# Low parts of weights by accumulating DMAs onto negated high parts

## The chip, the core and the metric

The kernel runs on one core of a Trainium2 chip. TensorE (PE), VectorE (DVE), ScalarE (ACT), GpSimd (POOL) and SyncE (SP) each run their own queue of instructions in order and wait for each other by semaphores; DMA queues move data between the device memory and the core. The metric is the time of one execution on the device in microseconds (us), as the median of several runs.

## What is computed

Two layers of an encoder over 768 tokens (512 of one request, 256 of another; the weights are shared) with 1024 channels. Each layer normalises its input, runs three token mixers on it, gates, projects and merges them, and adds the result:

```
h = rmsnorm(x, g_pre) * (1 + scale) + shift
cq, ckv, kr, gate_a, qkv_b, gate_b, qkv_c, gate_c, merge = split(h @ w_in)
p_a = (mla_attention(cq, ckv, kr, ...) * silu(gate_a)) @ w_pa        # branch A
p_b = (dilated_attention(rope(q_b), rope(k_b), v_b) * silu(gate_b)) @ w_pb   # branch B
p_c = (neighbourhood_attention(q_c, k_c, v_c, rpb) * silu(gate_c)) @ w_pc    # branch C
mg = sigmoid(merge)
mixed = mg[0] * p_a + mg[1] * p_b + mg[2] * p_c
x = x + gate * rmsnorm(mixed @ w_out, g_post)
```

All arrays are float32.

## The kernel before

Every product of two float32 matrices is made of three passes of PE on numbers rounded to float32r: high part times high part, weight's high part times activation's low part, weight's low part times activation's high part. The high part is the value rounded, the low part is what the rounding left off. So each weight tile needs a high and a low copy in SBUF before PE can use it.

`load_split` makes them. SP loads a raw tile of up to 1024 columns into one of three buffers (`WR`). Then, in pieces of 512 columns, ACT casts the piece into a slot `hi` of the ring `WH` (line 175), and `sub_lo` subtracts: `lo = raw - hi`, into a slot of the ring `WL` (line 158, the helper's line). Each ring has four slots of 512 columns, that is two full tiles. `sub_lo` goes to DVE, except that in some phases every n-th call goes to POOL: `LO_POOL = dict(l=2, m=3, p=1)` says every second call of phase "l" (latents of branch A), every third of "m" (branches B and C of the merge) and all of "p" (output projection). `sub_lo` also makes low parts of activations, so line 158 stands for more than weights: `lo<-ox` is the split of a branch's output in the merge.

A tile of a feature (`feat_mm`, line 199) is 48 matmuls: eight pieces of the contraction, three passes, two groups of tokens. Its products are named after the user: `qkb` (branch B), `qc` and `kc` (branch C), `gate`, `mg` (merge gates). `value_group` and `value_pair` (lines 722 and 741) make the values `vp`. In the merge each of 24 steps runs a merge gate `mg`, unless it was made ahead during the branches (`early`, then it is loaded back from `th_scr`), and 24 matmuls `pp` of the projection (line 1051), whose weights are one piece of 512 or 256 columns (`w_pj`). DVE multiplies the two (line 1060), POOL adds into `mixed` (line 1062). The merge of layer 0 also computes the conditioning vectors on DVE (`ada_tile`, line 309, on tiles `tm`).

The softmax of branches A and C (`soft_keys`) goes round the engines: DVE takes the maximum over the tiles (lines 650 and 652), POOL reduces it over the partitions (line 653), DVE subtracts (658), ACT takes the exponential (659), and the same for the sum. `pv` then splits the weights: ACT casts (667), DVE subtracts (668), PE multiplies with the values (671). Branch B does the same at lines 841 to 890.

The order on each engine is fixed when the kernel is built: a scheduler places the instructions of the program on the engines' queues, so that tiles of the next products are loaded and split under the current ones.

Of the kernel before, what the change touches and what calls it, by code (L numbers as in the profile page):

```python
# [15 lines left out]
AF = mybir.ActivationFunctionType  # L16
ALU = mybir.AluOpType
# [29 lines left out]
NW = (0, 64, 192, 256)  # L47


LO_POOL = dict(l=2, m=3, p=1)  # L50

FILL = ((2, 0, 1, 0, 2, 3, 1, 0, 1, 1, 1, 1, 0, 0, 0, 0, 0, 0, 0, 0, 0), (5, 0, 2, 3, 0, 4, 0, 1, 1, 1, 1, 2, 1, 0, 0, 0, 0, 0, 1, 0, 0))

# [10 lines left out]
def trunk_kernel(ctx, tc, x_t, c_row, c_col, w_ada0, w_ada, cols, w_a, w_feat, w_val, w_val2, w_uqk, w_qr, w_uv, w_pj, w_o,  # L64
                 bias_s, bias_p, rope_t, rope_k, mask_b, mask_c, y_t):
    nc = tc.nc
# [18 lines left out]
    def U(tag, dt=F32, name=None):  # L85
        return pool.tile([P, T], dt, tag=tag, name=name or tag, bufs=BUFS[tag])
# [11 lines left out]
    def ring(name):  # L98

        n, width = RINGS[name]  # L100
        t = part[name]
        state = dict(i=0)

        def take():
            i = state["i"]
            state["i"] = (i + 1) % n
            return t[:, i * width:(i + 1) * width]
        return take
# [8 lines left out]
    def Z4(name):  # L117
        return Z4_().rearrange("p (k g) -> p k g", g=2)

    def f(ap):  # L120
        return ap.bitcast(F32)
# [24 lines left out]
    state = dict(lo=0, pz=0, phase="l")  # L146
# [5 lines left out]
    def sub_lo(out, a, b, eng=None):  # L152

        if eng is None:
            state["lo"] += 1
            every = LO_POOL.get(state["phase"])
            eng = nc.gpsimd if every and state["lo"] % every == 0 else nc.vector
        eng.tensor_sub(out, a, b)  # L158

    def load_split(src, n, keep=None, ring=None):  # L160

        raw = WR()
        state["dma"] = nc.sync.dma_start(out=raw[:, :n], in_=src)
        parts = []
        w = 384 if keep else 1024 if ring else 512
        for o in range(0, n, w):
            m = min(w, n - o)
            if keep:
                t = U(keep, F32R)
                hi, lo = t[:, :w], t[:, w:]  # L170
            elif ring:
                hi, lo = ring(), ring()
            else:
                hi, lo = WH(), WL()
            nc.scalar.copy(hi[:, :m], raw[:, o:o + m])  # L175
            sub_lo(lo[:, :m], raw[:, o:o + m], f(hi[:, :m]))
            parts.append((hi, lo))
        return w // P, parts

# [386 lines left out]
    def branch_a(l, h_, h):  # L566
# [14 lines left out]
        for pr in range(4):  # L581
            early(l, h, FILL[l][1 + 2 * pr])
            if pr % 2 == 0:
# [17 lines left out]
                nc.scalar.activation(qr_hl[0], qr, AF.Copy, scale=scale)  # L601
                nc.vector.scalar_tensor_tensor(qr_hl[1], qr, scale, f(qr_hl[0]), ALU.mult, ALU.subtract)
            parts = load_split(w_uqk[l, pr], 640)
            qo = feat_mm(None, 3, cqn, name="qn", parts=parts)
            qn = []
# [575 lines left out]
    c = Z4("c")  # L1181
# [8 lines left out]
    for t_ in range(T // P):  # L1190
        x, x2 = U("cv", name="x"), x2s[t_ // 3][:, t_ % 3 * 256:t_ % 3 * 256 + 256]
        nc.sync.dma_start(out=x, in_=x_t[t_, :, :T])
        if t_ % 3 == 0:
            nc.sync.dma_start(out=x2s[t_ // 3].rearrange("p (t c) -> p t c", c=256),
                              in_=x_t[t_:t_ + 3, :, T:].rearrange("t p c -> p t c"))
# [208 lines left out]
```

## Time and profile before

| | |
|---|---|
| median of 3 runs | 1976.61 us (1974.0 to 1978.97) |
| profiled execution, its own time | 1972.72 us |
| span of the profile, first to last instruction | 1970.9 us |
| PE busy | 1848.2 us, 94% of the span |
| DVE busy | 1555.8 us, 79% |
| ACT busy | 1016.3 us, 52% |
| POOL busy | 645.1 us, 33% |

The profile gives, for one execution, when each instruction ran and what released it. Busy is the time in which an engine executed; what is left of the span is idle. The clock that TensorE was granted is 0.977 of its full speed as a mean. The stages below are cut at the places where the first matmuls of a branch begin; neighbouring branches overlap a little at the cuts.

### The profile page before, as it was taken

Reading aid. Unit: us, or ns where it says so; the run is one execution under the profiler, and the core shown is the slowest. Engines: PE = TensorE matmul, PEld = TensorE weight load, DVE = VectorE, ACT = ScalarE, POOL = GpSimd, SP = SyncE. Lnnn points to the kernel's source line nnn. Section 1 sums busy time; section 2 is a strip of 40 time slices with the busy share of each in tenths; the row PEclk is TensorE's granted clock in tenths of the full one; section 3 lists DMA queues with packets and bytes.
Section 4 is the critical chain, followed back from the end, with each engine's and each line's share of the span. In section 5 each row is a group of like instructions: output and inputs, shape, how many; then the busy total and the mean of one; then the engine's idle time right before and its main releaser. Section 6 shows DMA issues by size and latency. Waiting matters only on the chain.

```text
span 1970.9 us, 30150 instructions
## 1 busy us (share of the span) xinstructions
PE 1848.2 (94%) x10674; PEld 1641.7 (83%) x10674; DVE 1555.8 (79%) x3016; ACT 1016.3 (52%) x2121; POOL 645.1 (33%) x428
## 2 busy tenths in 40 slices
PE   7999899999989989998799999999999999988998
PEld 7987789988868878887699888889888878876898
DVE  8557779599978998999985258787699868997763
ACT  5456466456684555222364356574566674553241
POOL 6404334012121555026532014343022211454570
PEclk9999999999999989999899999999999999998999
DMA  8142231232212243557431332422323222233652
GB/s 294 65 125 73 81 118 62 92 101 79 92 46 97 79 145 118 192 171 241 143 132 52 103 118 87 136 82 68 105 76 94 84 70 97 87 105 100 210 180 70
DMA packets 94536, 220.20 MB, mean 112 GB/s; under 512 B 17984, under 2 KB 32392, under 8 KB 94384
## 3 DMA queue, kind: packets, MB, share of 16 engines
q1 hardware_dynamic: 89776, 211.97, 33.0%
q10 hardware_dynamic: 4608, 6.29, 1.1%
q8 instruction: 84, 1.38, 0.3%
q14 instruction: 68, 0.56, 0.1%
HBM read 172.73 MB, written 28.18 MB: 102 GB/s over the span
## 4 chain that ended last, share of the span: by engine, by line
PE 58%; DVE 24%; issue 6%; ACT 5%; DMA 4%; POOL 2%; SPq 0%; DVEq 0%; ACTq 0%; POOLq 0%
PE mg L199 15%; PE qkb L199 6%; PE op L1152 6%; PE vp L741 4%; PE pp L1051 4%; PE gate L199 4%; DVE fixed L668 3%; DVE fixed L158 3%; PE cq L547 3%; DVE fixed L309 2%; PE sp L632 2%; PE ck L547 2%; DVE tq L658 2%; PE vp L722 2%; PE qc L199 2%
## 5 line engine op out<-in xcount | busy, mean ns | idle before, releaser
L653 POOL PARTITION_ALL_REDUCE fixed<-fixed x128 | 305.5, 2413 | 516.0 <-DVE fixed L650 317.4
L199 PE MATMUL mg<-fixed 128*128 128x512 f32 (+1 forms) x2304 | 439.2, 343 | 0.7 <-DVE u L435 0.5
L199 PEld LDWEIGHTS mg<-fixed 128*128 128x128 f32 x2304 | 363.0, 192 | 52.0 <-DVE u L435 0.9
L175 ACT CAST fixed<-fixed 128x512 fp32r<-128x512 f32 (+1 forms) x332 | 199.3, 606 | 314.7 <-PE mg L199 103.8
L158 DVE TENSOR_TENSOR fixed<-fixed,fixed 128x512 fp32r<-128x512 f32 (+3 forms) x309 | 234.7, 764 | 96.5 <-ACT fixed L175 93.4
L199 PE MATMUL qkb<-fixed 128*128 128x512 f32 (+1 forms) x1152 | 211.5, 338 | 0.0
L199 PEld LDWEIGHTS qkb<-fixed 128*128 128x128 f32 x1152 | 176.9, 189 | 23.9
L199 PE MATMUL gate<-fixed 128*128 128x512 f32 (+1 forms) x960 | 185.5, 343 | 6.5 <-DVE fixed L158 4.4
L1051 PE MATMUL pp<-hi,fixed 128*128 128x512 f32 (+1 forms) x640 | 165.4, 347 | 8.9 <-DVE fixed L158 5.6
L199 PEld LDWEIGHTS gate<-fixed 128*128 128x128 f32 x960 | 150.5, 192 | 27.3 <-DVE fixed L158 4.9
L1051 PEld LDWEIGHTS pp<-hi,fixed 128*128 128x128 f32 x640 | 114.0, 195 | 26.4 <-DVE fixed L158 7.1
L668 DVE TENSOR_TENSOR fixed<-tq,fixed 128x512 fp32r<-128x512 f32 (+1 forms) x160 | 133.3, 855 | 1.5 <-ACT fixed L667 1.3
L659 ACT ACTIVATE tq<-tq 128x512 f32<-128x512 f32 (+1 forms) x160 | 83.4, 546 | 79.9 <-DVE tq L658 79.4
L1051 PE MATMUL pp<-lo,fixed 128*128 128x512 f32 (+1 forms) x320 | 110.8, 347 | 2.3 <-DVE lo L158 1.8
L658 DVE TENSOR_TENSOR tq<-tq,fixed 128x512 f32<-128x512 f32 (+1 forms) x160 | 100.3, 675 | 14.6 <-POOL fixed L653 14.2
L1152 PE MATMUL op<-wo,fixed 128*128 128x384 f32 (+1 forms) x648 | 108.6, 322 | 2.0 <-DVE fixed L1125 2.0
L309 DVE SCALAR_TENSOR_TENSOR fixed<-tm,fixed 128x768 f32<-128x768 f32 (+1 forms) x128 | 106.8, 834 | 2.0
L1152 PEld LDWEIGHTS op<-wo,fixed 128*128 128x128 f32 x648 | 103.0, 191 | 2.4 <-DVE fixed L1125 2.4
L424 POOL MEMSET kb<- 64x768 f32 x56 | 41.1, 735 | 166.5 <-PE sp L808 60.9
L856 POOL PARTITION_ALL_REDUCE fixed<-fixed x16 | 46.1, 2899 | 142.6 <-DVE fixed L833 75.2
L650 DVE TENSOR_TENSOR fixed<-tq 128x256 f32<-128x256 f32 (+1 forms) x128 | 78.2, 614 | 10.9 <-ACT tq L635 5.7
L667 ACT CAST fixed<-tq 128x512 fp32r<-128x512 f32 (+1 forms) x160 | 81.2, 531 | 8.8 <-PE o_ps L671 6.0
(244 smaller groups left out, 3884.9 us busy)
## 6 DMA issues: line engine op xcount, KB each, us to landing
fixed<-in_w_feat_dram SPq DMA_DIRECT2D x108, 512.0 KB
tm<-in_w_ada_dram SPq DMA_DIRECT2D x42, 384.0 KB
th_scr<-the SPq DMA_DIRECT2D x35, 384.0 KB
th<-th_scr SPq DMA_DIRECT2D x35, 384.0 KB
fixed<-in_w_val_dram SPq DMA_DIRECT2D x20, 512.0 KB
xs<-xb SPq DMA_DIRECT2D x96, 96.0 KB
fixed<-in_w_pj_dram SPq DMA_DIRECT2D x32, 256.0 KB
fixed<-in_w_o_dram SPq DMA_DIRECT2D x16, 512.0 KB
```

The costliest lines, as they stand in the source:

```text
L158: eng.tensor_sub(out, a, b)
L175: nc.scalar.copy(hi[:, :m], raw[:, o:o + m])
L199: state["mm"] = nc.tensor.matmul(outs[g], w[:, wsl], a[g], start=(i == 0 and wi == 0), stop=(i == nk - 1 and wi == 2))
L309: nc.vector.scalar_tensor_tensor(junk, x, 1.0, c, ALU.mult, ALU.mult, accum_out=ada2[:, l, i, g, j:j + 1])
L547: mm = nc.tensor.matmul(ps[t][c], hl[a][g][:, k, c0:c0 + P], w[k][c][b], start=(i == 0 and j == 0), stop=(i == KT - 1 and j == 2))
L653: nc.gpsimd.partition_all_reduce(red, out, P, RED.max if op == ALU.max else RED.add)
L658: nc.vector.tensor_sub(x, x, m)
L659: nc.scalar.activation(x, x, AF.Exp)
L667: nc.scalar.copy(hi, x)
L668: nc.vector.tensor_sub(lo, x, f(hi))
L1051: nc.tensor.matmul(pp, w[:, ws], o[k][a][:, o_:o_ + n], start=(i == 0), stop=(i == 3 * nk - 1))
L1152: mm = nc.tensor.matmul(op[cc], m[a][g][:, k, c0:c0 + P], parts[k][cc][b], start=(k == 0 and i == 0), stop=(k == KT - 1 and i == 2))
```

## The change

In the phases "b", "c", "m0" and "m" (branch B, branch C, first and later branches of the merge) a weight's low part is no longer made by `sub_lo`. ACT writes the negated rounded value, `lo = -raw`, rounded to float32r by the write, which is the negated high part. Then a DMA issued from POOL reads the same weights from the device memory a second time and adds them to `lo` in place, so that `lo = raw - hi`. ACT writes `hi` as before. The tiles with `keep` (output projection) and the other phases stay as they were. "m" leaves `LO_POOL`, so all `lo<-ox` are on DVE. The new names are line 178 (negation), 179 (the DMA) and 180 (cast); later lines are 7 higher than before.

```diff
--- before.py
+++ after.py
@@ -47,7 +47,9 @@
 NW = (0, 64, 192, 256)
 
 
-LO_POOL = dict(l=2, m=3, p=1)
+LO_POOL = dict(l=2, p=1)
+
+LO_DMA = ("b", "c", "m0", "m")
 
 FILL = ((2, 0, 1, 0, 2, 3, 1, 0, 1, 1, 1, 1, 0, 0, 0, 0, 0, 0, 0, 0, 0), (5, 0, 2, 3, 0, 4, 0, 1, 1, 1, 1, 2, 1, 0, 0, 0, 0, 0, 1, 0, 0))
 
@@ -172,8 +174,13 @@
                 hi, lo = ring(), ring()
             else:
                 hi, lo = WH(), WL()
-            nc.scalar.copy(hi[:, :m], raw[:, o:o + m])
-            sub_lo(lo[:, :m], raw[:, o:o + m], f(hi[:, :m]))
+            if not keep and state["phase"] in LO_DMA:
+                nc.scalar.activation(lo[:, :m], raw[:, o:o + m], AF.Copy, scale=-1.0)
+                nc.gpsimd.dma_start(out=lo[:, :m], in_=src[:, o:o + m], accum_op=ALU.add)
+                nc.scalar.copy(hi[:, :m], raw[:, o:o + m])
+            else:
+                nc.scalar.copy(hi[:, :m], raw[:, o:o + m])
+                sub_lo(lo[:, :m], raw[:, o:o + m], f(hi[:, :m]))
             parts.append((hi, lo))
         return w // P, parts
```

The lists of the built programs say what stands where. The old one has 309 weight subtractions of rings `WH` and `WL` on DVE: 288 of 128x512, 9 of 128x256, 4 of 128x384 and 8 of 128x128. In the new one 73 of 128x512 are left and none of 128x256, and POOL has 236 DMAs: 148 of `w_feat`, 40 of `w_val` (all 128x512) and 48 of `w_pj` (32 of 128x512, 16 of 128x256).

DVE in the merge of layer 0, between two steps (`fixed_72` holds the rounded tiles, `fixed_73` the plain ones; `tm` is the conditioning work). Before:

```order
L1060 SCALAR_TENSOR_TENSOR mixed<-th,pp 128x256
L309 SCALAR_TENSOR_TENSOR fixed_73<-tm,fixed_73 128x256
L158 TENSOR_TENSOR fixed_72<-fixed_73,fixed_72 128x512
L311 TENSOR_TENSOR fixed_73<-fixed_73 128x2
L309 SCALAR_TENSOR_TENSOR fixed_73<-tm,fixed_73 128x768
L309 SCALAR_TENSOR_TENSOR fixed_73<-tm,fixed_73 128x256
L309 SCALAR_TENSOR_TENSOR fixed_73<-tm,fixed_73 128x768
L309 SCALAR_TENSOR_TENSOR fixed_73<-tm,fixed_73 128x256
L158 TENSOR_TENSOR fixed_72<-fixed_73,fixed_72 128x512
L311 TENSOR_TENSOR fixed_73<-fixed_73 128x2
L309 SCALAR_TENSOR_TENSOR fixed_73<-tm,fixed_73 128x768
```
The same place in the changed kernel:

```order
L1067 SCALAR_TENSOR_TENSOR mixed<-th,pp 128x512
L316 SCALAR_TENSOR_TENSOR fixed_73<-tm,fixed_73 128x256
L316 SCALAR_TENSOR_TENSOR fixed_73<-tm,fixed_73 128x768
L1067 SCALAR_TENSOR_TENSOR mixed<-th,pp 128x256
L316 SCALAR_TENSOR_TENSOR fixed_73<-tm,fixed_73 128x256
L318 TENSOR_TENSOR fixed_73<-fixed_73 128x2
L316 SCALAR_TENSOR_TENSOR fixed_73<-tm,fixed_73 128x768
L316 SCALAR_TENSOR_TENSOR fixed_73<-tm,fixed_73 128x256
L316 SCALAR_TENSOR_TENSOR fixed_73<-tm,fixed_73 128x768
L316 SCALAR_TENSOR_TENSOR fixed_73<-tm,fixed_73 128x256
L318 TENSOR_TENSOR fixed_73<-fixed_73 128x2
```
The subtraction that stood between the conditioning rows (`L158`) is gone, and nothing stands in its place.

ACT in branch C of layer 0, in a stretch with the exponentials (line 659, later 666) and casts (667, later 674) of the softmax. Before:

```order
L175 CAST fixed_72<-fixed_73 128x512
L404 ACTIVATE qs<-qc_6817 64x64
L961 DMA fixed_73<-in_bias_p_dram 128x512
L659 ACTIVATE tq<-tq 128x512 x2
L667 CAST fixed_72<-tq 128x512 x2
L175 CAST fixed_72<-fixed_73 128x512
L416 CAST ka<-kc_6886 64x512
L417 CAST ka<-kc_6886 64x512
L416 CAST ka<-kc_6887 64x256
L417 CAST ka<-kc_6887 64x256
L659 ACTIVATE tq<-tq 128x256 x2
L667 CAST fixed_72<-tq 128x256 x2
L175 CAST fixed_72<-fixed_73 128x512
```
And a stretch of the same branch in the changed kernel:

```order
L666 ACTIVATE tq<-tq 128x512
L180 CAST fixed_72<-fixed_73 128x512
L178 ACTIVATE fixed_72<-fixed_73 128x512
L666 ACTIVATE tq<-tq 128x512
L674 CAST fixed_72<-tq 128x512 x2
L180 CAST fixed_72<-fixed_73 128x512
L178 ACTIVATE fixed_72<-fixed_73 128x512
L666 ACTIVATE tq<-tq 128x256 x2
L674 CAST fixed_72<-tq 128x256 x2
L180 CAST fixed_72<-fixed_73 128x512
L178 ACTIVATE fixed_72<-fixed_73 128x512
```
Each cast of a weight piece is followed, at once or some instructions later, by the negation `L178`; the scheduler has put the cast first.

POOL from the end of branch C to the merge of layer 1 (`L653`, later `L660`, are the softmax's all-reduces; a bare `ISA` row is a change of POOL's program). Before:

```order
L653 ISA fixed_73<-fixed_73 128x512
L653 ISA fixed_73<-fixed_73 128x256
L158 ISA
L158 TENSOR_TENSOR lo<-ox,hi 128x768
L653 ISA
L653 ISA fixed_73<-fixed_73 128x512
L653 ISA fixed_73<-fixed_73 128x256
L653 ISA fixed_73<-fixed_73 128x512 x2
L653 ISA fixed_73<-fixed_73 128x256 x2
L653 ISA fixed_73<-fixed_73 128x512
L653 ISA fixed_73<-fixed_73 128x256
L158 ISA
```
The changed kernel:

```order
L179 DMA fixed_72<-in_w_pj_dram 128x512
L660 ISA fixed_73<-fixed_73 128x512
L179 DMA fixed_72<-in_w_pj_dram 128x512
L660 ISA fixed_73<-fixed_73 128x256
L179 DMA fixed_72<-in_w_pj_dram 128x512
L660 ISA fixed_73<-fixed_73 128x512
L179 DMA fixed_72<-in_w_pj_dram 128x512
L660 ISA fixed_73<-fixed_73 128x256
L179 DMA fixed_72<-in_w_pj_dram 128x512 x2
L179 DMA fixed_72<-in_w_pj_dram 128x256 x5
L1069 ISA
L1069 TENSOR_TENSOR mixed<-mixed,th 128x768
```
The two changes of program around the single `lo<-ox` are gone, and a DMA stands between most of the all-reduces.

## Rows read from the trace of the kernel before

**Rows 1.** The page: span, busy time of the engines, the chain by engine.

```profile
span 1970.9 us, 30150 instructions
...
PE 1848.2 (94%) x10674; PEld 1641.7 (83%) x10674; DVE 1555.8 (79%) x3016; ACT 1016.3 (52%) x2121; POOL 645.1 (33%) x428
...
PE 58%; DVE 24%; issue 6%; ACT 5%; DMA 4%; POOL 2%; SPq 0%; DVEq 0%; ACTq 0%; POOLq 0%
```

**Rows 2.** B0, C0, M0, B1, C1, M1: length; busy PE, PEld, DVE, ACT, POOL; clock; DMA.

```profile
300.00:545.00 245.00, 238.58 (x1384) 213.63 (x1382) 209.23 (x365) 141.60 (x272) 53.31 (x32) 0.99 0.27 85
545.00:760.00 215.00, 193.15 (x1077) 165.34 (x1076) 191.17 (x349) 128.62 (x255) 81.10 (x42) 0.96 0.29 93
760.00:955.00 195.00, 172.85 (x941) 148.85 (x940) 184.32 (x388) 55.78 (x110) 76.92 (x43) 0.94 0.55 184
1320.00:1567.00 247.00, 240.19 (x1415) 215.19 (x1414) 211.79 (x368) 139.27 (x272) 58.73 (x32) 1.00 0.27 85
1567.00:1806.00 239.00, 216.80 (x1200) 185.16 (x1198) 193.32 (x353) 138.99 (x273) 78.69 (x42) 0.96 0.28 89
1806.00:1896.00 90.00, 85.48 (x475) 73.83 (x476) 73.84 (x104) 31.88 (x62) 54.86 (x34) 0.96 0.60 193
```

**Rows 3.** PE's waits in C0, C1 and M0: us, times, longest.

```profile
PE o_ps L671 <- DVE fixed L668: 4.9, 3, 1.9
...
PE o_ps L877 <- DVE fixed L158: 1.1, 3, 0.6
...
PE o_ps L671 <- DVE fixed L668: 8.9, 7, 2.1
PE o_ps L671 <- ACT fixed L667: 5.2, 1, 5.2
...
PE o_ps L671 <- DVE o_t L392: 0.6, 1, 0.6
...
PE op L1152 <- DVE th L1060: 12.1, 2, 11.4
PE pp L1051 <- DVE fixed L158: 5.6, 3, 2.0
```

**Rows 4.** Groups by line and shape, whole span: weight subtractions and casts.

```profile
L158 DVE TENSOR_TENSOR fixed<-fixed,fixed 128x512 fp32r<-128x512 f32 x288 | 223.8, 780 | 91.1 <-ACT fixed L175 88.1
L175 ACT CAST fixed<-fixed 128x512 fp32r<-128x512 f32 x300 | 184.7, 620 | 280.0 <-PE mg L199 89.5 <-PE qkb L199 45.5 <-DMA fixed<-in_w_pj_dram 27.4
...
L158 DVE TENSOR_TENSOR lo<-ox,hi 128x768 fp32r<-128x768 f32 x15 | 16.0, 1080 | 0.1
```

**Rows 5.** DVE's timeline in M0: start, us, then what.

```profile
885.58 0.41 DVE L158 TENSOR_TENSOR fixed<-fixed,fixed 128x256 fp32r<-128x256 f32 x1
...
889.79 2.02 DVE L158 TENSOR_TENSOR fixed<-fixed,fixed 128x256 fp32r<-128x256 f32 x1
```

**Rows 6.** POOL's timeline in M0 and at the end of C1.

```profile
889.00 2.53 POOL L1062 TENSOR_TENSOR mixed<-mixed,th 128x768 f32<-128x768 f32 x1 [1.30 <-DVE fixed L311]
...
1786.18 1.84 POOL L158 TENSOR_TENSOR lo<-ox,hi 128x768 fp32r<-128x768 f32 x1 [6.98 <-DVE fixed L678]
1794.50 2.87 POOL L653 PARTITION_ALL_REDUCE fixed<-fixed  x2 [6.48 <-issue]
```

**Rows 7.** The chain in order of time, in M0 and M1: start, us, what.

```profile
785.01 8.48 PE mg L199 x48
793.49 4.18 PE pp L1051 x24
...
1858.63 2.82 DMA fixed<-in_w_pj_dram
```

**Rows 8.** Groups of POOL in C0.

```profile
L653 POOL PARTITION_ALL_REDUCE fixed<-fixed x28 | 64.3, 2313 | 95.3 <-DVE fixed L650 89.8 <-DMA den_scr<-fixed 3.2 <-issue 1.6
```

**Rows 9.** The page's DMA queues: packets, MB, share of 16 engines.

```profile
q1 hardware_dynamic: 89776, 211.97, 33.0%
```

**Rows 10.** Groups of DVE in M0.

```profile
L158 DVE TENSOR_TENSOR fixed<-fixed,fixed 128x512 fp32r<-128x512 f32 x28 | 29.0, 1036 | 0.4 <-ACT fixed L175 0.4
```

## Prediction

> **What bounds the kernel now.** I read the page first: TensorE (PE) is busy 1848.2 us of a span of 1970.9 us, VectorE (DVE) 1555.8, ScalarE (ACT) 1016.3, GpSimd (POOL) 645.1 [rows 1]. The chain that ended last runs 58% through PE and 24% through DVE [rows 1]: PE is the bound, and where it stands still DVE mostly ends the wait. So at most PE's idle time can be won, and only in the stages that the change touches. I cut the span into stages (B is branch B, C branch C, M the merge, 0 and 1 the layers) and took length less PE busy [rows 2]: B0 6.4 us, C0 21.9, M0 22.2, B1 6.8, C1 22.2, M1 4.5, together 84 us. In the same rows DVE is busy 85% of B0, 89% of C0, 95% of M0, 86% of B1, 81% of C1 and 82% of M1, ACT never more than 60%. The reader is to see two kinds of stage: in B PE hardly waits although DVE is full; in C and at the end of M0 it waits for a full DVE. The waits say so [rows 3]: in C0 PE waits longest for the low part of the softmax weights (DVE L668, 4.9 us), in C1 too (8.9), and in M0 for the th product (DVE L1060) 12.1 and the weights' subtraction (DVE L158) 5.6. These low parts of weights (L158) rarely hold PE themselves; they take DVE's time ahead of work that does.
>
> **What goes.** DVE does 288 subtractions of 128x512 at 780 ns [rows 4]; by the order lists 73 are left, so 215 go: 167.7 us. Nine of 128x256 go too, some 0.41 us each [rows 5]: 4 us. The counter for POOL no longer exists in the merge, so 5 subtractions of lo<-ox come to DVE at 1.08 us [rows 4]: back 5 us. DVE loses 166 us, 11% of its work, all in the six stages. It also loses waits: L158 stood 91 us behind ACT's cast [rows 4], and everything on DVE behind it stood too (not all of it in these stages). POOL loses 17 subtractions (5 of 128x512, 7 of 128x256, 5 of lo<-ox), none longer than the 1.84 us of a lo<-ox [rows 6]: at most 31 us. And it loses two changes of program, the bare ISA rows in the order lists. One of them shows: at 1786.18 POOL does one lo<-ox of 1.84 us, and then stands 6.48 us, waiting for nothing that the profile names, before the two all-reduces that follow [rows 6]. PE waits 5.2 us for ACT in C1, once [rows 3], at 1799, behind those all-reduces.
>
> **What is added.** ACT negates 220 pieces of 128x512 and 16 of 128x256. The nearest row is its own cast, 620 ns [rows 4]; 236 of these are at most 146 us, and ACT goes from 52% to 59%. POOL issues 236 accumulating DMAs (B0 46, C0 32, M0 46, B1 50, C1 34, M1 28, counted from the tiles that each stage loads and summing to the list's 236). The trace has no DMA from POOL. What an issue holds POOL for lies between nothing (issues of SP and ACT are not counted as busy at all) and an all-reduce, 2.3 us [rows 8]; I take 1.2, the middle, since neither is nearer. The transfer is 256 KB. A plain one of that size stands for 2.82 us on the chain [rows 7]; this one also has to read the old content, so twice that, 5.6, is the upper end; I take 5, near the upper end. No DMA is added to SP's queue, which keeps its loads in a slightly altered order.
>
> **Is the low part in time?** A ring has four half tiles. PE takes 8.48 us for a tile of two halves and 4.18 for the merge's projection half [rows 7], so a slot that PE has freed is needed again after three others, 3 x 4.2 = 12.7 us. In that time now go the cast 0.62, the negation 0.62, the issue 1.2 and the landing 5: 7.4 us; with both upper ends 0.62 + 0.62 + 2.3 + 5.6 = 9.1. Both fit, with 3.6 to 5.3 us left for a queue on ACT or POOL. So where tile follows tile (all of B, most of M0) the transfers cost nothing: they lie under PE's own matmuls. That cover is gone where the raw load comes late: ACT waited 27.4 us for loads of w_pj [rows 4], in the merges. There a half is cast and used at once, and cast + subtraction = 1.4 us turns into 7.4. PE waited 5.6 us, 3 times, for L158 in M0 [rows 3]; each gets up to 6 us worse, 18 in all, of which I charge half, as the DVE that also held these products is freer.
>
> **The merge's DVE.** At 885.58 a subtraction of 128x256 takes 0.41 us, and the same at 889.79 takes 2.02 us [rows 5], while POOL adds two SBUF tiles into mixed from 889.00 for 2.53 us [rows 6]. So POOL's own subtractions cost DVE time as well, and they go; its adds stay. The open question is whether POOL's DMA issues slow DVE as its adds do. I count them as not, but if all 46 of M0 did, by the 1.61 us between those two rows, DVE would get back 74 us where it loses some 29 (28 subtractions of 128x512 at 1036 ns [rows 10]). The Trainium skill (SBUF — State Buffer, Who interferes with whom) has a rule for this: a DVE instruction with two SBUF inputs contends with a GpSimd instruction that reads SBUF, not with one that only writes. By that rule adds would slow DVE, as these rows agree, and issues, which write descriptors, would not; the term stays as counted.
>
> **Sum**, against the profiled execution's own 1972.7 us: C0 and C1, 44 us idle, of which 28 end on DVE (six kinds of wait in C0 from 4.9 us down to 1.1, four in C1 from 8.9 down to 0.6 [rows 3]). DVE loses 32 + 34 subtractions there, one for each DMA, at 0.78 us: 51 of 384 us busy, 13%, and the waits on the cast; I let half of the 28 go: -14. The program change at the end of C1: -6. M0: of 22 us, 15 go with the freer DVE and 9 come back by late loads: -6. B0 and B1, 13 us idle, a third: -4. M1: 0. ACT's 146 us lie mostly under idle time; a twentieth of them on the path of the softmax: +7, less 3 for DVE's freed waits: +4. Sum -26, so 1946.7. The median of the runs shown is 3.9 us above the profiled run: **1950 us**.
>
> **Rivals.** *More is won.* If DVE's queue was behind almost all of PE's waits, C gives 28 and M0 20: with the 6 and 4 it is -58, 1918. For it: DVE at 89 to 95%. Against: a softmax chain goes through DVE, POOL, DVE, ACT, DVE and PE in turn, and a wait in it does not vanish when DVE is free.
> *POOL becomes the queue* (slower). The order lists put a DMA straight before an all-reduce some 17 times in each C. Such a DMA waits for ACT's negation, which waits for PE to free the slot, and the all-reduce waits behind it, then DVE's tq, ACT's exp and PE's o_ps. At 2.3 us for 34 of them, 78 us; PE has gates and merge tiles to fill in with, so half is seen: +39. With -26 it is +13, 1990. It decides from 26 / 17 = 1.5 us of delay for each. For it: POOL's issues stand in line with the one engine that all heads pass. Against: POOL waits for DVE's partial results in C0 more than it works (64.3 us busy and 95.3 idle before these 28 all-reduces [rows 8]).
> *Landing is far longer than 5.6 us.* Above 12.7 - 2.4 = 10.3 us every half is late; at 11.5 us, 1.2 us for some 200 halves: +240, less the gain, 2190. Against: nothing in the trace takes so long.
> *It is hidden, or DMA eats it* (no change). The added 58.4 MB at the rate of the page (212 MB for 33.0% of the engines [rows 9]) are 9% of the span's DMA; M0 and M1 stand at 55% and 60% [rows 2], and 46 pieces in M0 add 10.7 MB to some 36, so it goes to 71%, and to 88% if each byte counts twice. If the loads of w_pj come so much later that ACT's 27.4 us double, that cancels the gain. The Trainium skill (Collectives: The Full Stack, The bandwidth ceiling) says that a DMA that adds needs two source reads and runs at about half the rate of a copy; by it the 88% holds. No row here has such a DMA.
>
> **How the numbers follow.** A difference of 0.3%, 6 us, is about what a measurement of this kernel can tell. Chances: the forecast (10 to 45 us won) 0.48; more won 0.13; no change 0.14; POOL's queue 0.18; late landing 0.07. Faster 0.61, same 0.14, slower 0.25. The range reaches up to the POOL rival and down to the larger gain, and leaves out the late landing and the tails: 1918 to 1992.
>
> **What would show it.** Right: 73 subtractions of 128x512 on DVE in place of 288, PE's idle in C0 and C1 each under 17 us, no 6.48 us gap on POOL at the end of C1, PE's waits for a DMA into fixed under 15 us in all. Wrong: PE waiting for lo from POOL's queue in B (then landing is long), POOL all-reduces that start late with DVE's partial result long done (POOL's queue), ACT's waits for w_pj far above 27 us (DMA), or DVE subtractions and adds of 2 us outside the merge's adds (the issues slow DVE).

## The result: slower by 1.2%

The changed kernel takes 2000.37 us (median of 4 runs, 1997.14 to 2004.62), the kernel before 1977.79 (4 runs beside them, 1974.0 to 1980.24). The ratio is 1.0119, 95% interval 1.0101 to 1.0136. That is outside the range, on its slow side. The profiled execution took 2001.39 us.

The page of the changed kernel: busy time, DMA queues, chain, groups of instructions, DMA issues (KB each, median us to landing).

```profile
span 1999.6 us, 30560 instructions
...
PE 1860.8 (93%) x10674; PEld 1641.9 (82%) x10674; DVE 1417.6 (71%) x2797; ACT 1135.7 (57%) x2357; POOL 809.9 (41%) x647
...
q1 hardware_dynamic: 89776, 211.97, 32.8%
q0 software_dynamic: 33984, 59.78, 18.2%
...
PE 32%; DVE 12%; DMA 6%; ACT 5%; issue 4%; POOL 2%; SPq 1%; ACTq 0%; DVEq 0%; POOLq 0%
...
L179 POOL DMA_DIRECT2D fixed<-in_w_feat_dram x148 | 131.0, 899 | 373.6 <-ACT fixed L178 247.2
...
L178 ACT ACTIVATE fixed<-fixed 128x512 fp32r<-128x512 f32 (+1 forms) x236 | 145.3, 616 | 26.9 <-PE vp L748 23.8
...
fixed<-in_w_feat_dram POOLq DMA_DIRECT2D x148, 256.0 KB, 4.7
...
fixed<-in_w_val_dram POOLq DMA_DIRECT2D x40, 256.0 KB, 5.0
```

Against [rows 1] VectorE gave back 138 us (166 were predicted; without the DMAs, in e4_no_dma below, it is 152), ScalarE took 119 more, and PE is busy 12.6 us *longer* with the same 10674 matmuls. The new queue q0 takes 18.2% of the DMA engines for 59.78 MB; q1 takes 32.8% for 211.97, so each added byte costs the engines twice what a byte on q1 does. The prices that the prediction took were near: POOL is held 0.90 us by an issue (1.2 taken), a negation takes 616 ns (620), a transfer lands after 4.7 to 5.0 us (5).

PE's waits (us, times, longest), whole span; these answer to [rows 3]:

```profile
PE o_ps L678 <- DVE fixed L675: 29.2, 27, 3.2
PE pp L1058 <- DMA fixed<-in_w_pj_dram: 16.6, 6, 7.9
...
PE pp L1058 <- DVE th L1067: 6.8, 1, 6.8
PE o_ps L897 <- ACT fixed L893: 6.4, 10, 1.5
```

and DVE's:

```profile
DVE xb L460 <- DMA xs<-xb: 41.1, 12, 12.8
DVE o_t L650 <- DMA den<-rden_scr: 40.5, 8, 10.9
...
DVE fixed L685 <- DMA fixed<-den_scr: 27.7, 8, 5.2
...
DVE o_t L1007 <- DMA den<-rden_scr: 26.0, 7, 7.7
```

In the kernel before:

```profile
DVE o_t L643 <- DMA den<-rden_scr: 26.4, 7, 5.1
...
DVE fixed L678 <- DMA fixed<-den_scr: 10.4, 8, 2.1
DVE o_t L1000 <- DMA den<-rden_scr: 7.5, 3, 3.6
...
DVE xb L453 <- DMA xs<-xb: 6.8, 4, 2.1
```

All are small transfers between SBUF and device memory or within SBUF: `xs` is the exchange of halves in the rotation of queries and keys (lines 457 and 458; four transfers of 96 KB for each tile), `den` and `den_scr` the round trip of the softmax's sums. The rise is only in part the new DMAs' doing. With the DMAs left out (e4_no_dma below) the same four already stand at:

```profile
DVE o_t L649 <- DMA den<-rden_scr: 34.0, 8, 7.7
DVE xb L459 <- DMA xs<-xb: 30.2, 10, 10.4
...
DVE o_t L1006 <- DMA den<-rden_scr: 20.6, 8, 5.6
...
DVE fixed L684 <- DMA fixed<-den_scr: 15.4, 9, 2.5
```

With the subtractions gone VectorE stands longer before the same transfers, whatever the DMAs do. So how long a transfer takes says more than how long VectorE waits for it. PE hardly waits for the new low parts, except in the merge.

### The profile page after: what moved, and what is told of

Read it like the earlier page. It is cut to its first block, busy times and chain, and to the rows that moved or that the text cites. A ratio compares the mean times of both kernels' runs of the same rounds, so it can differ in the third digit from the quotient of the medians.

```text
span 1999.6 us, 30560 instructions
## 1 busy us (share of the span) xinstructions
PE 1860.8 (93%) x10674; PEld 1641.9 (82%) x10674; DVE 1417.6 (71%) x2797; ACT 1135.7 (57%) x2357; POOL 809.9 (41%) x647
## 3 DMA queue, kind: packets, MB, share of 16 engines
q1 hardware_dynamic: 89776, 211.97, 32.8%
q0 software_dynamic: 33984, 59.78, 18.2%
## 4 chain that ended last, share of the span: by engine, by line
PE 32%; DVE 12%; DMA 6%; ACT 5%; issue 4%; POOL 2%; SPq 1%; ACTq 0%; DVEq 0%; POOLq 0%
PE mg L206 10%; PE op L1159 6%; PE pp L1058 5%; PE qkb L206 2%; DVE fixed L316 2%; DVE fixed L675 2%; DMA xs<-xb 2%; PE gate L206 2%; PE cq L554 1%; DVE tq L665 1%; PE ck L554 1%; PE sp L639 1%; DMA den<-rden_scr 1%; DMA fixed<-in_w_pj_dram 1%; DVE fixed L657 1%
## 5 line engine op out<-in xcount | busy, mean ns | idle before, releaser
L660 POOL PARTITION_ALL_REDUCE fixed<-fixed x128 | 303.7, 2392 | 352.9 <-DVE fixed L657 172.9
L206 PE MATMUL mg<-fixed 128*128 128x512 f32 (+1 forms) x2304 | 433.1, 340 | 1.3 <-DMA fixed<-in_w_feat_dram 1.1
L206 PEld LDWEIGHTS mg<-fixed 128*128 128x128 f32 x2304 | 358.2, 190 | 52.4 <-DMA fixed<-in_w_feat_dram 1.7
L179 POOL DMA_DIRECT2D fixed<-in_w_feat_dram x148 | 131.0, 899 | 373.6 <-ACT fixed L178 247.2
L1058 PE MATMUL pp<-hi,fixed 128*128 128x256 f32 (+1 forms) x640 | 168.5, 350 | 24.9 <-DMA fixed<-in_w_pj_dram 16.6
L178 ACT ACTIVATE fixed<-fixed 128x512 fp32r<-128x512 f32 (+1 forms) x236 | 145.3, 616 | 26.9 <-PE vp L748 23.8
L316 DVE SCALAR_TENSOR_TENSOR fixed<-tm,fixed 128x768 f32<-128x768 f32 (+1 forms) x128 | 111.4, 870 | 5.6 <-DMA tm<-in_w_ada_dram 3.2
L665 DVE TENSOR_TENSOR tq<-tq,fixed 128x512 f32<-128x512 f32 (+1 forms) x160 | 106.1, 710 | 5.8 <-POOL fixed L660 5.4
L160 DVE TENSOR_TENSOR fixed<-fixed,fixed 128x512 fp32r<-128x512 f32 (+2 forms) x85 | 57.0, 678 | 57.5 <-ACT fixed L182 55.7
```

The costliest lines, as they stand in the source:

```text
L178: nc.scalar.activation(lo[:, :m], raw[:, o:o + m], AF.Copy, scale=-1.0)
L179: nc.gpsimd.dma_start(out=lo[:, :m], in_=src[:, o:o + m], accum_op=ALU.add)
L206: state["mm"] = nc.tensor.matmul(outs[g], w[:, wsl], a[g], start=(i == 0 and wi == 0), stop=(i == nk - 1 and wi == 2))
L316: nc.vector.scalar_tensor_tensor(junk, x, 1.0, c, ALU.mult, ALU.mult, accum_out=ada2[:, l, i, g, j:j + 1])
L660: nc.gpsimd.partition_all_reduce(red, out, P, RED.max if op == ALU.max else RED.add)
L665: nc.vector.tensor_sub(x, x, m)
```

## Experiments

Each run is timed beside the kernel before, whose medians lie between 1975.4 and 1978.9. Differences between two kernels are therefore taken from the ratios, times 1978 us; "over before" is (ratio - 1) x 1978. By the intervals each such value is good to 2 to 4 us, and a difference of two rows to 3 to 5 us.

| run | median us | ratio to before, 95% | over before |
|---|---|---|---|
| changed kernel | 2000.37 | 1.0119 (1.0101 to 1.0136) | +23.5 |
| e7_pool | 1961.31 | 0.9917 (0.9904 to 0.9929) | -16.4 |
| e4_no_dma | 1935.67 | 0.9794 (0.978 to 0.9809) | -40.7 |
| e6_narrow | 1955.25 | 0.9887 (0.9875 to 0.99) | -22.4 |
| e5_plain | 1973.85 | 0.9979 (0.9969 to 0.999) | -4.2 |
| e12_beside | 2022.55 | 1.0236 (1.0221 to 1.0251) | +46.7 |
| e15_sbuf | 1993.15 | 1.0091 (1.0076 to 1.0106) | +18.0 |
| e8_not_merge | 1992.1 | 1.0084 (1.0066 to 1.0102) | +16.6 |
| e10_b_only | 1974.06 | 0.9994 (0.9984 to 1.0005) | -1.2 |
| e9_c_only | 1977.1 | 1.0001 (0.9992 to 1.001) | +0.2 |
| e11_m_only | 1982.2 | 1.0031 (1.002 to 1.0041) | +6.1 |
| e20_b_narrow | 1955.41 | 0.988 (0.9865 to 0.9895) | -23.7 |
| e19_c_narrow | 1961.44 | 0.9925 (0.9909 to 0.9941) | -14.8 |
| e18_m_narrow | 1969.43 | 0.9963 (0.9948 to 0.9979) | -7.3 |
| e17_no_exchange | 1950.94 | 0.9865 (0.9849 to 0.9881) | -26.7 |
| e16_b_no_exchange | 1966.71 | 0.9945 (0.9932 to 0.9957) | -10.9 |
| e21_b_plain_noex | 1961.05 | 0.9907 (0.9891 to 0.9924) | -18.4 |
| e13_adds | 1988.67 | 1.0068 (1.0051 to 1.0085) | +13.5 |
| e14_pool_adds | 1956.14 | 0.99 (0.9887 to 0.9913) | -19.8 |

The theories: **traffic** (the added transfers occupy the DMA engines, and small transfers come late), **GpSimd's queue** (issues, waits for ScalarE and changes of program stand ahead of other work), **ScalarE** (its 236 negations), **landing** (the low part itself is late for PE), **order** (the scheduler's other order of the program, which changes with most of these edits).

### The change taken apart

The part without DMAs, in the kernel before:

```diff
-LO_POOL = dict(l=2, m=3, p=1)
+LO_POOL = dict(l=2, p=1)
```

> The kernel before with only the entry for the merge taken out of the table of GpSimd's subtractions, so that VectorE makes all low parts of the merge: the part of the change that has nothing to do with DMAs. The prediction's step expects the 6.48 us gap of GpSimd at the end of branch C in layer 1 to go, and 3 to 8 us to be won: 1970 to 1975 us. A rival expects VectorE, 95% busy in the merge of layer 0, to lose that again: 1976 to 1984 us.

It won 16.4 us, twice the most that was expected. The windows of the last merge, from the first `pp` to the last (length; busy PE, PEld, DVE, ACT, POOL; clock; DMA), before:

```profile
1782.80:1896.20 113.40, 101.69 (x559) 87.67 (x558) 85.50 (x121) 38.36 (x75) 65.05 (x38) 0.94 0.53 167
```

and with the entry gone:

```profile
1782.90:1884.10 101.20, 97.62 (x558) 84.77 (x557) 80.47 (x131) 37.98 (x75) 53.93 (x30) 1.00 0.59 189
```

It lies here: this stage is 12.2 us shorter, where the two spans differ by 10.9. Of the 12.2 PE's idle time is 8.1 and its busy time 4.1, with a granted clock of 1.00 in place of 0.94. PE's idle time before was mostly three waits for `o_ps` between 1794 and 1809, of 5.17, 2.02 and 2.04 us, behind the all-reduces that followed two changes of POOL's program; none of them is left. The 17 subtractions that POOL loses in the same edit were not tested apart from the changes of program.

Then the DMAs, in the changed kernel. Left out:

```diff
-nc.gpsimd.dma_start(out=lo[:, :m], in_=src[:, o:o + m], accum_op=ALU.add)
```

> The changed kernel with the accumulating DMAs left out: the low part stays the negated high part, so the addition of the weights is not computed; ScalarE still negates, VectorE still has no subtraction. The queue orders shift somewhat, since the scheduler no longer sees the DMAs. Theory traffic (the added bytes delay the small transfers that branches A, B, C wait for) and theory GpSimd queue (issue plus waiting for ScalarE ahead of the all-reduces) both expect the loss to be gone and the relief of VectorE to be left: 1945 to 1965 us. Theory ScalarE (the 236 negations in ScalarE's queue cost the time) expects 1990 to 2000 us, as changed. Theory order (the scheduler's other order of the program costs the time) expects no value; about 1980 if the relief is worth nothing.

Cut to 8 columns:

```diff
-nc.gpsimd.dma_start(out=lo[:, :m], in_=src[:, o:o + m], accum_op=ALU.add)
+nc.gpsimd.dma_start(out=lo[:, :8], in_=src[:, o:o + 8], accum_op=ALU.add)
```

> The changed kernel with each accumulating DMA cut to its first 8 columns (128 rows of 32 B, 4 KB in place of 256 KB); the other columns of the low part stay the negated high part, so most of the addition is not computed. Number of DMAs, of rows in them, their waits on ScalarE and ScalarE's work stay; a third or so of the order lists differs. Theory traffic expects 1945 to 1970 us, as without DMAs. Theory GpSimd queue expects 1995 to 2003, as changed. Theory ScalarE expects 1990 to 2000.

Made plain:

```diff
-nc.gpsimd.dma_start(out=lo[:, :m], in_=src[:, o:o + m], accum_op=ALU.add)
+nc.gpsimd.dma_start(out=lo[:, :m], in_=src[:, o:o + m])
```

> The changed kernel with plain DMAs in place of the accumulating ones: the low part becomes the raw weight, so the subtraction is not computed. The same instructions in the same order on every queue; only the old content is no longer read. Theory traffic expects the added DMA share to fall from 18% to about 9%, and so about half of the loss against a kernel without DMAs to go: 1975 to 1988 us, with the waits for xs and den shorter. Theory GpSimd queue expects 1996 to 2003 us, since issue and wait for ScalarE stay; theory ScalarE and theory order the same 1996 to 2003. Theory landing (the low part itself comes late for TensorE) expects the waits for w_pj at pp to fall and some 5 to 8 us won: 1992 to 1995.

Without the DMAs the kernel is 24.3 us faster than e7_pool, and 9 us below the least that was expected: that is what VectorE's relief is worth in this other order of the program, with all of ScalarE's negations in it, so theory ScalarE falls. The small DMAs cost 18.3 us, the plain ones 18.2 more, the accumulating ones another 27.7. The last step has the same instructions in the same order on every queue, so order can't make it; only the reading of the old content differs. In the other steps the order changes too. The page of e5_plain:

```profile
q0 software_dynamic: 33984, 59.78, 11.3%
...
fixed<-in_w_feat_dram POOLq DMA_DIRECT2D x148, 256.0 KB, 3.8
```

Where it goes, by stages of the five profiles (cut where `qkb`, C's `vp` and `pp` begin and where the last `pp` ends; length against the kernel in the column before it):

| stages | relief (e7 to e4) | issue and queue (e4 to e6) | traffic (e6 to changed) |
|---|---|---|---|
| A0 to the first `qkb`, B0, B1 | -2.3 | -4.1 | +22.6 |
| C0, C1 | -9.4 | -1.7 | +11.4 |
| M0 to the next `qkb`, M1 | -13.6 | +25.6 | +12.1 |

So issue and queue are paid in the merges alone, and traffic everywhere, most of it in B. Each column holds a change of the program's order too, the third in its part from narrow to plain, and no run took it apart. The step from plain to accumulating alone, which has none, is 10.1 us in A0, B0 and B1, 9.3 in C0 and C1 and 10.1 from M0 on.

Is it that PE gets the low parts late? As many DMAs of the same size beside the old subtractions, from the raw tile into a scratch in device memory that nobody reads:

```diff
-nc.scalar.activation(lo[:, :m], raw[:, o:o + m], AF.Copy, scale=-1.0)
-nc.gpsimd.dma_start(out=lo[:, :m], in_=src[:, o:o + m], accum_op=ALU.add)
+state["side"] = state.get("side", -1) + 1
+nc.gpsimd.dma_start(out=side_scr[state["side"] % 4][:, :m], in_=raw[:, o:o + m], accum_op=ALU.add)
 nc.scalar.copy(hi[:, :m], raw[:, o:o + m])
+sub_lo(lo[:, :m], raw[:, o:o + m], f(hi[:, :m]))
```

> All subtractions stay on VectorE, as in the kernel at 1961.3 us; beside them GpSimd issues the same number of accumulating DMAs of the same size from the raw tile into a scratch in device memory that nobody reads, so that TensorE never waits for what such a DMA writes, ScalarE negates nothing, and VectorE is not relieved. What is added is traffic, GpSimd's issue time, and a raw tile held some us longer. Theory traffic with theory GpSimd queue expects the whole cost that the changed kernel has over the one without DMAs, 40 to 65 us: 2000 to 2026 us. Theory landing (the low part comes too late for TensorE) and theory ScalarE expect 1961 to 1970.

63.1 us over e7_pool, where the changed kernel is 64.2 over e4_no_dma: DMAs cost as much where PE waits for none of them and ScalarE negates nothing, so neither landing nor ScalarE is needed for a sum of this size. That the two are so close is in part luck, since they do not pay in the same places. Here the queue takes 21.0% of the engines, a raw tile is held until its DMA has read it, and VectorE still has its subtractions; by the stages it costs 10.5 us up to the end of B0 and in B1, 15.0 in C and 36.4 from M0 on, where the changed kernel pays 18.5, 9.7 and 37.7 over e4_no_dma. The same bytes with SBUF as the source:

```diff
-in_=src[:, o:o + m], accum_op=ALU.add)
+in_=raw[:, o:o + m], accum_op=ALU.add)
```

> The changed kernel with the accumulating DMAs reading the weights from the raw tile in SBUF instead of a second time from device memory; the result is the same. The DMA engines move as many bytes, the device memory gives 60 MB less, and a raw tile is held until the DMA has landed. Theory traffic, in the form that the time of the DMA engines counts, expects no change or a little more: 1997 to 2006 us, share of the queue near 18%. In the form that the device memory's rate counts: 1965 to 1985.

5.5 us less, a little below what was expected, in another order of the program; the queue still takes 17.4% of the engines. So most of the cost does not come from the second reading of the device memory.

### Where: B, C or the merges

`LO_DMA` with ("b", "c"), ("b",), ("c",) or ("m0", "m"), and each of the last three with 8 columns as in e6_narrow:

> The changed kernel with the DMAs in branches B and C alone; in the merge VectorE subtracts, and GpSimd does none of it (as in the run without the merge's entry in the table, 1961.3 us). By the stages of that run and of the changed kernel, branch B with the end of branch A before it costs 16 us in the two layers and branch C nothing, the merges 24 us. Theory traffic (the added bytes delay the small transfers of branch B) expects the 16 us to stay: 1972 to 1982 us. Theory GpSimd queue (the merge's DMAs stand behind GpSimd's change of program and its adds) alone expects the loss to be gone: 1955 to 1965.

> The same with the DMAs in branch B alone. Theory traffic expects all of the 16 us of B and of the end of A: 1972 to 1982 us, and the rotated halves of queries and keys to land some 3.7 us after their issue, where they land after 1.7 us without these DMAs. Theory GpSimd queue expects 1958 to 1965, since B has few instructions on GpSimd.

> The same with the DMAs in branch C alone. By the stages C has no net cost: 1957 to 1966 us, with the wait of TensorE for the softmax weights' low part little changed. If the relief of VectorE in C were worth the prediction's 14 us it would be 1944 to 1950. If GpSimd's all-reduces of the softmax are held up by the DMAs in front of them (theory GpSimd queue, in the form of the prediction's rival), 1975 or more.

> The DMAs in the merges alone; branches B and C as before, GpSimd without subtractions in the merge. Theory GpSimd queue (the DMAs of the last merge stand behind GpSimd's change of program and its adds) expects a cost over the 1961.3 us of the kernel without DMAs of 8 to 16 us, as between the kernel with DMAs in B and C (1992) and the changed one (2000): 1968 to 1978. If the relief of VectorE in the merges (10 us in the first, 3 in the second by the kernel without DMAs) outweighs it: 1950 to 1960.

> The DMAs in branch B alone (1974.1 us), each cut to its first 8 columns (most of the addition not computed). Number, issue, waits and ScalarE's negations stay. Theory traffic expects the 13 us over the kernel without DMAs to go, and VectorE's relief to show: 1952 to 1964 us. If ScalarE's queue or GpSimd's issues cost B its time: 1970 to 1978.

> The DMAs in branch C alone (1977.1 us), each cut to its first 8 columns (most of the addition not computed). Number of DMAs ahead of the all-reduces, their issue time and their waits on ScalarE stay. Theory traffic expects the 16 us over the kernel without DMAs to go and VectorE's relief to show: 1948 to 1962. The prediction's rival, GpSimd's queue ahead of the all-reduces, expects 1972 to 1980.

> The DMAs in the merges alone (1982.2 us), each cut to its first 8 columns (4 KB in place of 256 KB, most of the addition not computed). Theory GpSimd queue expects the wait for the weights behind GpSimd's change of program, some 7 us at once, and most of the 21 us to stay: 1972 to 1982. Theory traffic expects most of it to go: 1952 to 1964.

Over e7_pool: B 15.2 us, C 16.6, merges 22.5; B with C 33.0. B came out as expected. e8_not_merge and e11_m_only are above everything that was expected, and e9_c_only came out where the theory of GpSimd's queue had put it: C alone has a cost of its own that the stages of the whole change did not show. With 8 columns it is B -7.3, C +1.6, merges +9.1. So traffic alone is 22.5 us in B, 15.0 in C and 13.4 in the merges, 50.9 in all (45.9 in the whole change). In the pair for B the two programs have almost the same order: SyncE's queue is the same, and the others differ in about one instruction of a hundred. In C up to a tenth differs. e18_m_narrow lies between what its two theories expected. In C the DMAs ahead of the all-reduces, their issues and their waits stay in e19_c_narrow, and all but 1.6 us of the cost is gone. The relief of C, 9.4 us by the stages, doesn't show there either, so GpSimd's queue ahead of the softmax costs some 11 us at most; in the whole change the stages show none of it (-1.7).

### How traffic reaches PE in B

One exchange in branch B, SP's issues and DVE's instruction that needs the result. Changed kernel, SP:

```profile
400.77 0.59 SPq L458 DMA_DIRECT2D xs<-xb  x1
```

and DVE:

```profile
405.21 0.69 DVE L460 TENSOR_TENSOR xb<-xb,fixed 128x512 f32<-128x512 f32 x1 [5.49 <-DMA xs<-xb]
```

The same with narrow DMAs, SP and DVE:

```profile
397.49 0.59 SPq L458 DMA_DIRECT2D xs<-xb  x1
```

```profile
399.88 0.69 DVE L460 TENSOR_TENSOR xb<-xb,fixed 128x512 f32<-128x512 f32 x1 [2.08 <-DMA xs<-xb]
```

From the end of the last issue (401.36 and 398.08) to DVE's start it is 3.85 us against 1.80. Over all exchanges that DVE waited for, the median is 1.7 us before (4 of them) and without DMAs (10), 1.8 with narrow ones (12), 3.1 with plain ones (10) and 3.7 with accumulating ones (12; 3.7 in e10_b_only too, as expected there). The reads of `den`, counted in the same way, slow less: 3.0 us before, 3.1 with narrow DMAs, 3.6 with accumulating ones. What follows on PE (windows of the changed kernel: length; busy PE, PEld, DVE, ACT, POOL; clock; DMA):

```profile
409.80:412.30 2.50, 0.08 (x2) 0.03 (x1) 2.32 (x3) 2.43 (x4) 0.00 (x0) 0.89 0.72 177
412.30:415.00 2.70, 2.70 (x13) 2.70 (x13) 1.27 (x3) 1.94 (x4) 0.42 (x1) 0.50 0.03 6
...
418.00:432.00 14.00, 14.00 (x83) 12.36 (x82) 9.05 (x18) 8.25 (x19) 6.09 (x6) 1.00 0.66 139
```

```profile
412.27 0.79 PE L815 MATMUL sp<-qs,ka 128*128 128x256 f32 x2 [2.42 <-ACT ka L424]
```

PE waits 2.42 us for the rotated keys' cast, and then runs 13 matmuls, 2.73 us to 415.00, at the lower of its two clocks, 1.2 GHz. With narrow DMAs it does the same work there without a wait, in 1.44 us:

```profile
408.00:409.44 1.44, 1.44 (x14) 1.44 (x13) 0.64 (x2) 0.68 (x2) 0.46 (x1) 1.00 0.05 11
```

So the wait costs half as much again, 1.29 us of slower matmuls, and this part counts as busy.

Is the exchange the path? Left out, with and without DMAs in B:

```diff
-for b in range(0, P, 2 * half):
-    nc.sync.dma_start(out=xs[b:b + half], in_=x[b + half:b + 2 * half])
-    nc.sync.dma_start(out=xs[b + half:b + 2 * half], in_=x[b:b + half])
 for o, n in GROUPS:
+    nc.vector.tensor_mul(xs[:, o:o + n], x[:, o:o + n], sin[:, :n])
     nc.vector.tensor_mul(x[:, o:o + n], x[:, o:o + n], cos[:, :n])
-    nc.vector.tensor_mul(xs[:, o:o + n], xs[:, o:o + n], sin[:, :n])
```

> Control: the kernel without DMAs for weights (1961.3 us), rotations without the exchange of halves (left out of the computation). 1945 to 1960 us, since VectorE waits 7 us in all for those transfers and ScalarE for what follows.

> The DMAs in branch B alone (1974.1 us), and the rotations of queries and keys computed without the exchange of halves, which two transfers from SBUF to SBUF make for each tile in branch B (the exchange is left out of the computation). To be read against the next run, which has no DMAs for weights. Theory traffic through small transfers that come late expects most of branch B's cost of 13 us to go with them: 0 to 6 us above the next run, what is left being the end of branch A. If the DMAs cost B something else (ScalarE's negations, GpSimd's queue, TensorE waiting for low parts), the difference stays 10 to 15 us.

> The kernel with the DMAs in branch B alone and without the exchange of halves (1966.7 us, control without DMAs 1950.9), with plain DMAs in place of accumulating ones, so that the old content is not read (the subtraction is not computed): the same instructions in the same order. If traffic costs branch B its time by another path than the exchange transfers, some 5 to 9 us go: 1957 to 1962. If the 15.8 us that were left without the exchange are not traffic: 1964 to 1968.

The expectation failed: B still pays 15.8 us, as much as with the exchange (15.2). With plain DMAs 7.5 of them go, which is what the last of these expectations gave for traffic that takes another path than the exchange. By the stages, plain to accumulating costs B0 and B1 9.4 us with the exchange (182.3 to 187.4, 203.6 to 207.9) and 1.1 without (185.1 to 185.6, 201.7 to 202.3), each pair in one order (the pair without the exchange has its DMAs in B alone). So in the branch itself the step from plain to accumulating goes mostly through the exchange; the rest of the 7.5 lies in other stages, mainly between the end of M0 and B1 (3.3 us, where `den` is fetched). What else B pays without the exchange, 11.9 us in B0 and B1 against e17_no_exchange, stays open: those two programs have different orders. The exchange is thus one path of the traffic in B, and not shown to be the main one.

In C, from plain to accumulating, DVE's waits for `den`, `den_scr` and the bias of branch C grow from 7.3 to 13.4 us in C0 and from 8.9 to 14.4 in C1, while the two stages grow by 5.1 and 4.2. That fits small transfers as the path there too, but no run took them out.

### The merges

POOL at the start of the last merge, changed kernel (in brackets the idle time before, and what ended it):

```profile
1864.47 0.86 POOL L179 DMA_DIRECT2D fixed<-in_w_pj_dram  x1 [8.31 <-ACT fixed L180]
1875.27 1.79 POOL L1069 TENSOR_TENSOR mixed<-mixed,th 128x768 f32<-128x768 f32 x1 [9.94 <-issue]
1877.02 1.04 POOL L179 DMA_DIRECT2D fixed<-in_w_pj_dram  x1
```

ACT's negation for the piece of the last row, and PE:

```profile
1864.38 0.41 ACT L178 ACTIVATE fixed<-fixed 128x256 fp32r<-128x256 f32 x1
```

```profile
1881.01 1.22 PE L1058 MATMUL pp<-hi,fixed 128*128 128x512 f32 x2 [7.94 <-DMA fixed<-in_w_pj_dram]
```

Before its first addition POOL changes its program (the bare `ISA` row of L1069) and does nothing for 9.94 us that the profile names. The DMA whose negation ended at 1864.79 is issued after that and after one addition, at 1877.02, and PE, which stood 7.94 us for it, goes on at 1881.01. In M0 POOL stands 8.01 us in the same way at 803.9, with a DMA of `w_feat` behind it. The additions moved to VectorE, in the changed kernel and in e7_pool:

```diff
-nc.gpsimd.tensor_add(mixed[j], mixed[j], th)
+nc.vector.tensor_add(mixed[j], mixed[j], th)
```

> The changed kernel with the 32 additions into the merged result on VectorE in place of GpSimd. So GpSimd's change of program in the last merge comes after all but one of the merge's DMAs. Theory GpSimd queue expects TensorE's waits for the merge's weights (16.6 us, 7.9 at once) to fall to a few us and 8 to 15 us to be won: 1985 to 1993 us. Theory traffic alone, without such a queue, expects 1998 to 2004.

> Control for the run before it: the same move of the 32 additions to VectorE in the kernel without DMAs (1961.3 us). TensorE has no wait for a DMA to lose there and VectorE gets some 30 us of work more in the merges: 1960 to 1970 us. If it gains as much as the move does in the changed kernel, the gain there is not the queue's.

10.0 us won, as expected, but 3.4 also in the control, which came out 4 us below its expectation: 6.6 are left for the queue, barely clear of the noise of four ratios. PE's waits for `w_pj` fall only from 16.6 to 11.6 us, not to the few that were expected. So the change of program probably has a share; the rest of the merges' 25.6 us of issue and queue was not taken apart. The control, e14_pool_adds, is the fastest kernel with the full computation: ratio 0.99 (0.9887 to 0.9913).

## Why the prediction was wrong, step by step

- **What bounds the kernel, what goes.** Right: PE is the bound, and less work on VectorE wins 24.3 us. By stages C gave 9.4 (14 predicted), the merges 13.6 (15 and 0), B and the end of A 2.3 (4). 73 subtractions of 128x512 are left. ScalarE's +4 was not measured apart; it lies within the 24.3.
- **POOL's change of program, -6.** Right in kind, the size off: 16.4 by the ratio, 10.9 by the two profiles. The step took the one wait of 5.2 us for what the gap cost PE; two more waits went with it, and 4.1 us of matmuls at the lower clock.
- **"So where tile follows tile (all of B, most of M0) the transfers cost nothing: they lie under PE's own matmuls."** This step failed. It asked only whether the low part is in time, and it mostly is: its numbers held; outside the merge's projection PE waits 3.9 us in all for them. It did not ask what else uses the DMA engines. Charged 0, the traffic measured 22.5 us in B and 15.0 in C. One path of it is shown: an exchange has nothing to hide under, it slows from 1.7 to 3.7 us, and DVE, then ACT, then PE wait; with the exchange left out, the step from plain to accumulating costs B0 and B1 1.1 us in place of 9.4. By what path the rest is paid is not shown.
- **The merges, 9 us for late loads.** The mechanism is another. ACT's waits for raw `w_pj` fell; it is POOL's queue that is late (issue and queue 25.6 us, of which the change of program is the part that shows) and traffic (12.1 by the stages). Those waits, before and in the changed kernel:

```profile
ACT fixed L175 <- DMA fixed<-in_w_pj_dram: 29.7, 9, 6.5
```

```profile
ACT fixed L180 <- DMA fixed<-in_w_pj_dram: 8.5, 3, 3.8
```

- **The sum.** -26 was forecast. Measured: -16.4 (POOL's table), -24.3 (relief), +18.3 (issue and queue), +45.9 (traffic, 27.7 of it with the order unchanged), which is +23.5.
- **Rivals.** POOL's queue was placed ahead of the all-reduces, at 39 us; there it costs some 11 at most (e19_c_narrow), and nothing by the stages. It is real in the merges, where the prediction did not look. "DMA eats it" had the right resource and the wrong victim: the loads of `w_pj` instead of small transfers, and by bytes it gave 9% of the engines (for 58.4 MB; they are 59.78) where the added queue takes 18.2%. M0 went to 82%, between its 71% and its 88%:

```profile
757.00:964.40 207.40, 183.46 (x1007) 156.82 (x1005) 174.75 (x388) 83.36 (x165) 100.72 (x75) 0.97 0.82 227
```

  The Trainium skill (Collectives: The Full Stack, The bandwidth ceiling) says of the adding step of a collective that it needs two source reads and so runs at about half the rate of a copy; the same bytes took 18.2% against 11.3% as plain DMAs here, 1.61 times. Landing above 10.3 us: did not happen.
- **Issues don't slow VectorE.** Right. The subtractions of 128x512 in e12_beside, where they stand beside the DMAs, and in e7_pool:

```profile
L161 DVE TENSOR_TENSOR fixed<-fixed,fixed 128x512 fp32r<-128x512 f32 x293 | 244.3, 837 | 99.5 <-ACT fixed L184 51.0 <-ACT fixed L181 45.5
```

```profile
L158 DVE TENSOR_TENSOR fixed<-fixed,fixed 128x512 fp32r<-128x512 f32 x293 | 225.2, 772 | 89.2 <-ACT fixed L175 85.1 <-PE sp L632 1.3
```

The means differ by 65 ns, but not by the issues: in e12_beside the 41 that run beside a DMA issue and nothing else on POOL take 682 ns as a mean, the 155 with nothing beside them 686. The slow ones stand beside an all-reduce or an addition, a few with an issue as well.
- **What would show it.** From the first `vp` of C to the first `pp`, PE's idle time is 17.7 us in C0 and 14.2 in C1 (under 17 each was the sign, by a cut that takes in a little more). By the same cut it was 23.5 and 10.5 before, so C0 gained and C1 did not. Before, C0 and C1, then changed:

```profile
539.40:745.80 206.40, 182.86 (x1011) 155.84 (x1010) 182.63 (x335) 127.07 (x251) 74.35 (x39) 0.96 0.28 90
1588.40:1782.80 194.40, 183.92 (x1017) 157.29 (x1018) 170.33 (x316) 114.63 (x233) 67.96 (x36) 0.97 0.27 91
```

```profile
552.80:757.00 204.20, 186.52 (x1003) 157.80 (x1003) 151.76 (x282) 137.86 (x271) 91.65 (x71) 0.95 0.54 133
1607.20:1804.40 197.20, 183.05 (x1023) 155.59 (x1022) 146.17 (x275) 135.18 (x273) 98.18 (x75) 0.99 0.61 142
```

  The 6.48 us gap is gone from the end of C1, and one of 9.94 stands in the merge. PE's waits for a DMA into `fixed` are 20.5 us (under 15 was the sign).

Open stay the path of traffic in C, what issue costs in the merges besides the change of program, the 11.9 us of B without the exchange, and how much of each step but the last is the other order of the program.

## What to carry to other kernels

Work that is moved from an engine onto DMA is not hidden because its own result is in time: list the small transfers that some engine waits for with nothing to do, and ask what they cost when the DMA engines are twice as busy. Count an accumulating DMA by the time it takes on the engines, not by its bytes. Before DMAs go on GpSimd's queue, look for its changes of program, since everything behind one waits.

## What the runs showed of the hardware

- An exchange by transfers of 96 KB within SBUF was there 1.7 us after the last issue had ended. It took 3.7 us while another queue kept accumulating DMAs in flight, and 3.1 us with plain ones.
- After PE had stood for 2.42 us the granted clock was 0.50 for 2.7 us, and 13 matmuls took 2.73 us in place of 1.44.
- After a change of program POOL stood 6.48, 8.01 and 9.94 us where the profile names nothing else that it waited for; a DMA issue behind one waited too.
- A DMA issue holds POOL for 0.90 us, and a subtraction on VectorE beside it takes 682 ns, as with nothing beside it (686).
- Issued by POOL, an accumulating DMA of `w_feat` of 4 KB lands after 3.0 us, one of 256 KB after 4.7, a plain one of 256 KB after 3.8 (medians). As accumulating DMAs the same bytes take 1.61 times the time of the DMA engines that they take as plain ones.
